# A Mamba-2 and attention trunk on one core: the first group's xs turned by TensorE, and a later place for the second group's turn

## The chip, the cores and the metric

The kernel runs on one NeuronCore of a Trainium2 chip. A core has five engines with a queue each: TensorE (PE in the profile; its weight loads are PEld), VectorE (DVE), ScalarE (ACT), GpSimd (POOL) and SyncE (SP, which only starts DMAs here). Each engine takes its instructions in the order of its queue, and waits for others by semaphores. Matrix products are written to PSUM and must be read from there by DVE or ACT before their buffer is used again. The metric is the device time of one execution in microseconds (us), lower is better; the time of a kernel is the median of its runs.

## The reference

One Mamba-2 layer and one sliding-window attention layer, 256 tokens of width 2048, float32. The change lies in the Mamba-2 layer. Cut to it:

```python
zxbcdt = x @ w_in                      # z, xs, B, C, dt
xbc = silu(conv(xbc) + conv_b)         # 4 taps, for xs, B and C
dt  = softplus(dt_raw + dt_bias)
x_c = xs * dt[..., None]               # tokens x (64 heads x 64), in 8 groups of 8 heads
cb     = einsum("bcqgn,bcsgn->bgcqs", c_c, b_c)
y_diag = einsum("bgcqs,bgrcqs,bcsgrp->bcqgrp", cb, decay_in, x_c)
y = y_diag + y_off + xs * d_skip
y = y * silu(z)
y = y * rsqrt(mean(y * y over the 512 channels of a group) + EPS) * norm_w
h = y @ w_out
x = layernorm(ALPHA * x + h)
```

The sum over `s` (tokens) needs x_c with tokens on the partitions. The projection leaves xs with channels on the partitions, so each group's xs must be turned.

## The kernel before, in words

**Products.** Every weight is split into a high and a low part (`wh` by ACT, L164; `wl` by DVE, L167), x likewise, and a product is three matmuls (L252). Weights come in units of 128 x 2048: SyncE loads two halves into raw buffers `wr`, ACT and DVE split them (`load_unit`, `split_half`), and `next_unit` keeps the loads two units ahead. A raw buffer is free when both splits have read it.

**Groups and blocks.** There are eight groups of ten blocks (`group`, `block`). A block is 48 matmuls into one of four PSUM buffers (`mm`). In group 0 the blocks are z0, z1, z2, b, c, xs0 to xs3, z3; in the others b, c, xs0 to xs3, z0 to z3. So blocks 10, 11 and 12 are bt, ct and xs0 of group 1, and 16 to 19 its z. Each b, c or xs block goes through `conv_silu`: one ACT instruction and three DVE (L492, L494) out of PSUM, a Tanh (L497) and a product (L498). A z block is one ACT (L582) and one DVE (L583) out of PSUM.

**The state-space part of a group.** `cb` makes B times C (L590, L591) and masks it (L592). The decays `e` come from a broadcast load (`load_decay`), from ACT (L549, L557) and a product with cbm on DVE (`by_cb`, L597). `ymm` multiplies e with `xd`, the turned and scaled xs (L631), and DVE takes the result out of PSUM with `el` (L636) and adds the skip (L642). `gate` multiplies by z, squares and sums on GpSimd (L647, L649, L653), and ACT and DVE split y into yH and yL (L661, L662). `norm` sums the squares over the partitions on TensorE (L671); group 0 then takes the root with small DVE instructions (L680 to L687).

**The turn of xs.** `turn_xs` transposes 32 x 32 pieces on DVE, four instructions of 128 x 256 (L604). `carry_xs` moves the pieces to their partitions with 16 ACT copies (L613). `scale_xs` multiplies by dt (L618).

**The output product.** `out_units(g - 1, ...)` runs behind some blocks of group g (`OUT_AT`): for each unit and each half of the tokens 12 matmuls of 512 columns into an `mm` buffer (L323 to L325), which DVE scales by r and adds into `xr` (L332). For group 0 these stand behind blocks 16, 17, 18 and 19.

**The order.** The program is written in blocks. `plan` holds what comes behind a block, `between` what comes behind a block's matmuls but ahead of its evictions; the numbers count blocks from the start (`at(t, fn, ...)`). A scheduler may move instructions within an engine's queue, but those marked `keep_in_program_order` (through `pinned`) keep their order. `visits` names the functions that put other work on TensorE; the block behind one takes its first slice of x from its usual place and not from a copy.

Of the kernel before, what the change touches and what calls it, by code (L numbers as in the profile page):

```python
# [8 lines left out]
F32 = mybir.dt.float32  # L9
# [5 lines left out]
ALU = mybir.AluOpType  # L15
AX = mybir.AxisListType

P = 128
S = 256
# [64 lines left out]
def trunk(ctx: ExitStack, tc: tile.TileContext, A: dict, out: bass.AP, dbg=None):  # L84
    nc = tc.nc
    PSUM = bass.MemoryType.PSUM

    def pool(name, bufs=1, side=None, space=None, stack=ctx):
        kw = {"space": space} if space is not None else {}
        return stack.enter_context(  # L90
            tc.tile_pool(name=name, bufs=bufs, side=side, reuse_waits="tile", **kw)
        )
# [9 lines left out]
    def nm(s):  # L102
        uid[0] += 1
        return f"{s}_{uid[0]}"

    def mm_tile():
        return mm_ps.tile([P, 512], F32, tag="mm", name=nm("mm"), bufs=4)

    def ax_tile():
        return ax_ps.tile([P, 512], F32, tag="ax", name=nm("ax"), bufs=4)  # L110

    cc = cst.tile([P, 1024], F32, tag="cc", name="cc")
    ident = cc[:, 0:128]
# [169 lines left out]
    ap = pool("ap", stack=w_stack)  # L283
# [25 lines left out]
    def pinned(m, pin):  # L309
        if pin:  # L310
            tc.keep_in_program_order(m)
# [86 lines left out]
    dtx = ap.tile([P, 2, NHD], F32, tag="dtx", name="dtx")  # L398
# [163 lines left out]
    gs = [G() for _ in range(NG)]  # L562
# [32 lines left out]
    def by_cb(g, hf):  # L595
        e = es[g, hf]
        nc.vector.tensor_tensor(e[:], e[:], gs[g].cbm[:].unsqueeze(1).to_broadcast([P, 4, 384]), ALU.mult)  # L597

    def turn_xs(g):

        st = gs[g]
        st.zx = ap.tile([P, 4, 8, 32], F32, tag="yz", name=nm("zx"), bufs=1)
        for i in range(4):
            nc.vector.transpose(st.zx[:, i].rearrange("p f b -> p (f b)"), st.xs[i][:])  # L604
        st.xd = ap.tile([P, 2, 4, P], F32, tag="xd", name=nm("xd"), bufs=1)

    def carry_xs(g, js):
# [103 lines left out]
        else:  # L711
            (in_b, in_c)[k](g, ps)

    visits = (turn_dt, cb, ymm, norm)

    def group(g):
        for b in range(10):
# [75 lines left out]
    between = {}  # L793
# [6 lines left out]
    def at(t, fn, *a):  # L800
        plan.setdefault(t, []).append((fn, *a))
# [5 lines left out]
    for g in range(NG):  # L807
        t = 10 * g
        if g == 0:
            at(TD, turn_dt, *dts)  # L810
            at(4, load_decay, 0, 1)
            at(8, load_low, 0)
            pos = dict(cb=CB0, y=13)

            xs_at = 9
            halves = [(5, 6, 7), (7, 8, 9)]
            by = (9, 10)
        elif g == 1:
            at(10, load_decay, 1, 0)
            at(10, load_decay, 1, 1)  # L820
            at(15, load_low, 1)
            pos = dict(cb=6, y=Y_AT, norm=10 + CB_AT)

            halves = [(13, 14, 15), (15, 16, 16)]
            by = (16, 17)
        else:
            at(t - 5, load_decay, g, 0)
            at(t - 5, load_decay, g, 1)
            at(t, load_low, g)
            steps = t - 1  # L830
            pos = dict(cb=CB_AT, y=Y_AT, norm=10 + CB_AT)
        for hf in range(2):
            if g < 2:
                sa, sb, ex = halves[hf]
                if (g, hf) != (1, 0):
                    at(sa, sum_decay, g, hf, 0, 2)
                at(sb, sum_decay, g, hf, 2, 4)
            else:
                at(steps + hf, sum_decay, g, hf)
                ex = steps + 1 + hf  # L840
            at(ex, exp_decay, g, hf)
        if g == 1:
            at(16, norm, 0)
        at(t + pos["cb"], cb, g)
        for hf in range(2):
            at(by[hf] if g < 2 else t + pos["cb"] + hf, by_cb, g, hf)
        if g > 0:
            xs_at = t + 6
        at(xs_at, turn_xs, g)
        if g == 0:  # L850
            at(9, carry_xs, 0, (0,))
            between[10] = [(carry_xs, 0, (1,))]
            between[11] = [(carry_xs, 0, (2, 3)), (scale_xs, 0)]
        else:
            for n, js in enumerate(((0,), (1,), (2, 3)) if g < 2 else ((0, 1), (2, 3))):
                at(xs_at + n, carry_xs, g, js)
            at(xs_at + 2, scale_xs, g)
        at(t + pos["y"], ymm, g)
        if g == 0:
            at(t + pos["y"], sum_decay, 1, 0, 0, 2)  # L860
        for i in range(4):
            at(t + pos["y"], gate, g, i)
        if g > 0:
            at(t + pos["norm"], norm, g)
# [148 lines left out]
    for h in range(2):  # L1013
        ps = mm_tile()
# [449 lines left out]
```

## Time and profile before

| | us |
|---|---|
| median of 3 runs | 986.46 |
| lowest, highest | 985.95, 986.79 |
| profiled execution, its own time | 985.89 |
| its span, first to last instruction | 984.1 |

The granted TensorE clock was 0.999 of full speed. In the profile L12 means line 12 of the kernel. In a timeline a row gives the start from the beginning of the span, the duration, the engine, the line and operation, output<-inputs, shapes, the number of instructions merged, and in brackets the engine's idle time just before and what ended it. Durations of neighbouring instructions overlap; the pace of an engine is the distance between starts. In a row of groups the busy time and the mean in ns of one instruction follow the bar, then the idle time before them. A list of waits has the total, the number and the longest.

### The profile page before, as it was taken

Reading aid. Unit: us, or ns where it says so; the run is one execution under the profiler, and the core shown is the slowest. Engines: PE = TensorE matmul, PEld = TensorE weight load, DVE = VectorE, ACT = ScalarE, POOL = GpSimd, SP = SyncE. Lnnn points to the kernel's source line nnn. Section 1 sums busy time; section 2 is a strip of 40 time slices with the busy share of each in tenths; the row PEclk is TensorE's granted clock in tenths of the full one; section 3 lists DMA queues with packets and bytes.
Section 4 is the critical chain, followed back from the end, with each engine's and each line's share of the span. In section 5 each row is a group of like instructions: output and inputs, shape, how many; then the busy total and the mean of one; then the engine's idle time right before and its main releaser. Section 6 shows DMA issues by size and latency. Waiting matters only on the chain.

```text
span 984.1 us, 18075 instructions
## 1 busy us (share of the span) xinstructions
PE 973.6 (99%) x7004; PEld 883.8 (90%) x7004; DVE 783.3 (80%) x1202; ACT 662.7 (67%) x1236; POOL 103.2 (10%) x137
## 2 busy tenths in 40 slices
PE   9999899999999999999999999999999999999998
PEld 8999889999998999999999999888898978978976
DVE  7888897876878787797788687989867678766786
ACT  7596787667676666657766667467467777764772
POOL 0000403004003000300300300303100000000003
PEclk9999999999999999999999999999999999999999
DMA  9798467566657656656656564648655546464542
GB/s 359 251 292 297 147 230 255 174 208 200 214 172 241 212 190 219 209 169 236 204 175 198 176 216 149 211 166 281 220 163 165 190 157 196 159 208 147 200 143 86
DMA packets 61557, 198.89 MB, mean 202 GB/s; under 512 B 6848, under 2 KB 11360, under 8 KB 61216
## 3 DMA queue, kind: packets, MB, share of 16 engines
q1 hardware_dynamic: 58528, 188.53, 58.0%
q0 software_dynamic: 2336, 8.69, 2.7%
q8 instruction: 55, 0.90, 0.4%
q10 hardware_dynamic: 608, 0.52, 0.2%
q14 instruction: 30, 0.25, 0.1%
HBM read 195.49 MB, written 2.23 MB: 201 GB/s over the span
## 4 chain that ended last, share of the span: by engine, by line
PE 86%; DVE 5%; ACT 4%; DMA 3%; issue 1%; SPq 1%; ACTq 0%; DVEq 0%
PE mm L252 43%; PE mm L984 11%; PE mm L323 9%; PE mm L325 9%; PE mm L324 9%; PE ax L631 2%; DVE wl L167 2%; DMA wr<-in_wa 1%; ACT wh L164 1%; ACT e L549 1%; DMA rb<-rscr 1%; DMA xr<-in_first 1%; ACT xd L613 1%; PE ax L1124 1%; SPq L192 1%
## 5 line engine op out<-in xcount | busy, mean ns | idle before, releaser
L167 DVE TENSOR_TENSOR wl<-wr,wh 128x1024 fp32r<-128x1024 f32 (+2 forms) x338 | 392.8, 1181 | 88.5 <-ACT wh L164 86.6
L164 ACT ACTIVATE wh<-wr 128x1024 fp32r<-128x1024 f32 (+2 forms) x338 | 332.1, 1010 | 92.4 <-PE mm L252 32.7
L252 PE MATMUL mm<-xH,wh 128*128 128x256 f32 x1280 | 355.0, 277 | 0.0
L252 PE MATMUL mm<-xL,wh 128*128 128x256 f32 x1280 | 354.2, 277 | 0.0
L252 PE MATMUL mm<-xH,wl 128*128 128x256 f32 x1280 | 354.0, 277 | 0.0
L252 PEld LDWEIGHTS mm<-xH,wh 128*128 128x128 f32 x1280 | 240.8, 188 | 2.0 <-ACT wh L198 0.3
L252 PEld LDWEIGHTS mm<-xL,wh 128*128 128x128 f32 x1280 | 240.6, 188 | 0.9
L252 PEld LDWEIGHTS mm<-xH,wl 128*128 128x128 f32 x1280 | 240.6, 188 | 0.0
L323 PE MATMUL mm<-wh,yH 128*128 128x512 f32 x256 | 101.3, 396 | 2.4 <-DVE xr L332 2.4
L324 PE MATMUL mm<-wh,yL 128*128 128x512 f32 x256 | 99.8, 390 | 0.0
L325 PE MATMUL mm<-wl,yH 128*128 128x512 f32 x256 | 99.7, 389 | 0.0
L647 POOL TENSOR_TENSOR yz<-yz,z 128x256 f32<-128x256 f32 x32 | 32.7, 1030 | 469.6 <-DVE yz L642 469.6
L494 DVE SCALAR_TENSOR_TENSOR cv<-mm,pc,cv 128x255 f32<-128x255 f32 x144 | 68.4, 476 | 4.5 <-ACT cv L492 3.1
L252 PE MATMUL mm<-x1H,wh 128*128 128x256 f32 x256 | 71.9, 281 | 0.0
L252 PE MATMUL mm<-x1L,wh 128*128 128x256 f32 x256 | 71.1, 278 | 0.0
L252 PE MATMUL mm<-x1H,wl 128*128 128x256 f32 x256 | 71.1, 278 | 0.0
L984 PE MATMUL mm<-wh,x1H 128*128 128x512 f32 x160 | 63.1, 394 | 0.0
L984 PE MATMUL mm<-wl,x1H 128*128 128x512 f32 x160 | 61.8, 389 | 0.0
L984 PE MATMUL mm<-wh,x1L 128*128 128x512 f32 x160 | 60.9, 390 | 0.0
L323 PEld LDWEIGHTS mm<-wh,yH 128*128 128x128 f32 x256 | 48.1, 188 | 13.0 <-DVE xr L332 2.8
L497 ACT ACTIVATE xs<-cv 128x256 f32<-128x256 f32 x32 | 13.3, 415 | 66.8 <-DVE cv L494 66.8
L325 PEld LDWEIGHTS mm<-wl,yH 128*128 128x128 f32 x256 | 48.1, 188 | 10.2
(228 smaller groups left out, 1456.1 us busy)
## 6 DMA issues: line engine op xcount, KB each, us to landing
wr<-in_wa SPq DMA_DIRECT2D x154, 512.0 KB, 5.2
wr<-in_wo SPq DMA_DIRECT2D x64, 512.0 KB, 4.4
wr<-in_wq SPq DMA_DIRECT2D x32, 512.0 KB, 4.5
wr<-in_wg SPq DMA_DIRECT2D x31, 512.0 KB, 5.0
wr<-in_wb SPq DMA_DIRECT2D x16, 512.0 KB, 4.3
wr<-in_wb SPq DMA_DIRECT2D x32, 256.0 KB, 3.8
rb<-rscr SPq DMA_DIRECT2D x11, 512.0 KB, 4.1
wr<-in_wkv SPq DMA_DIRECT2D x8, 512.0 KB, 4.8
```

The lines of the kernel that those rows point to most:

```text
L164: m = nc.scalar.activation(h[:, sl], v, AF.Copy)
L167: m = nc.vector.tensor_tensor(l[:, sl], v, h[:, sl].bitcast(F32), ALU.subtract)
L192: nc.sync.dma_start(raw, A["first"][:, k, :])
L252: m = nc.tensor.matmul(ps, a, b, start=first and i == 0, stop=last and i == 2)
L323: pinned(nc.tensor.matmul(ps, aH[:, k, hs], u.h[:, ks], start=k == 0 and add is None, stop=False), pin)
L324: pinned(nc.tensor.matmul(ps, aL[:, k, hs], u.h[:, ks], start=False, stop=False), pin)
L325: pinned(nc.tensor.matmul(ps, aH[:, k, hs], u.l[:, ks], start=False, stop=k == 3), pin)
L494: nc.vector.scalar_tensor_tensor(a[:, sft:], ps[:, : S - sft], w(3 - sft), a[:, sft:], ALU.mult, ALU.add)
L497: nc.scalar.activation(dst, a[:], AF.Tanh)
L631: nc.tensor.matmul(ps[64 * r : 64 * r + 64, cols], st.xd[:, c, i, 64 * r : 64 * r + 64], e[:, 256:] if c else e[:, :256], start=c == 0, st ...
L647: nc.gpsimd.tensor_tensor(v, v, st.z[i][:], ALU.mult)
L984: m = nc.tensor.matmul(ps[:], (x1H, x1L, x1H)[i][:, kk, hs], (u.h, u.h, u.l)[i][:, ks], start=(kk, i) == (0, 0), stop=ui == 3 and (k, i) = ...
```

## The change

Group 0's `turn_xs`, `carry_xs` and `scale_xs` (behind blocks 9, 10 and 11) go. In their place `turn_first(0)` stands behind the matmuls of block 11: eight 128 x 128 transposes on TensorE into two PSUM buffers, and four DVE instructions that multiply by dt on the way out of PSUM, kept in program order. In group 1 `turn_xs` moves from behind block 16 to between the matmuls and the eviction of block 17, its four transposes kept in program order, and the 16 copies come in two parts behind blocks 17 and 18 in place of three behind 16, 17 and 18. Groups 2 to 7 keep their places. In DVE's built queue group 1's four transposes stand behind the first two L332 and two splits of weights, where before they stood ahead of these L332; the first e product of group 1 stands between the two L332.

```diff
+    def turn_first(g):
+        st = gs[g]
+        st.xd = ap.tile([P, 2, 4, P], F32, tag="xd", name=nm("xd"), bufs=1)
+        for k in range(2):
+            ps = ax_tile()
+            for i in (2 * k, 2 * k + 1):
+                for c in range(2):
+                    o = (i % 2) * S + c * P
+                    nc.tensor.transpose(ps[:, o : o + P], st.xs[i][:, c * P : (c + 1) * P], ident)
+            for i in (2 * k, 2 * k + 1):
+                o = (i % 2) * S
+                hh = g * 8 + 2 * i
+                m = nc.vector.tensor_tensor(
+                    st.xd[:, :, i, :].rearrange("p c (h d) -> p c h d", h=2),
+                    ps[:, o : o + S].rearrange("p (c h d) -> p c h d", c=2, h=2),
+                    dtx[:, :, hh : hh + 2].unsqueeze(3).to_broadcast([P, 2, 2, 64]), ALU.mult,
+                )
+                pinned(m, True)
...
         for i in range(4):
-            nc.vector.transpose(st.zx[:, i].rearrange("p f b -> p (f b)"), st.xs[i][:])
+            m = nc.vector.transpose(st.zx[:, i].rearrange("p f b -> p (f b)"), st.xs[i][:])
+            pinned(m, g == 1)
...
-    visits = (turn_dt, cb, ymm, norm)
+    visits = (turn_dt, cb, turn_first, ymm, norm)
...
-            xs_at = 9
+            between[11] = [(turn_first, 0)]
...
         if g > 0:
             xs_at = t + 6
-        at(xs_at, turn_xs, g)
-        if g == 0:
-            at(9, carry_xs, 0, (0,))
-            between[10] = [(carry_xs, 0, (1,))]
-            between[11] = [(carry_xs, 0, (2, 3)), (scale_xs, 0)]
-        else:
-            for n, js in enumerate(((0,), (1,), (2, 3)) if g < 2 else ((0, 1), (2, 3))):
-                at(xs_at + n, carry_xs, g, js)
+            if g == 1:
+                between[17] = [(turn_xs, 1)]
+            else:
+                at(xs_at, turn_xs, g)
+            for n, js in enumerate(((0, 1), (2, 3))):
+                at(xs_at + n + (g == 1), carry_xs, g, js)
             at(xs_at + 2, scale_xs, g)
```

## The prediction

> **What bounds the kernel now.** I read the busy shares and the chain of waits first, then TensorE's own waits, then the timeline of each engine round them.
>
> ```profile
> PE 973.6 (99%) x7004; PEld 883.8 (90%) x7004; DVE 783.3 (80%) x1202; ACT 662.7 (67%) x1236; POOL 103.2 (10%) x137
> ...
> PE 86%; DVE 5%; ACT 4%; DMA 3%; issue 1%; SPq 1%; ACTq 0%; DVEq 0%
> ```
> TensorE (PE) is the bound. An instruction added to it costs its whole pace, and only its idle time can be won. The list of its waits over the span is short:
>
> ```profile
> PE ax L671 <- POOL sq L653: 2.6, 1, 2.6
> PE mm L323 <- DVE xr L332: 2.4, 1, 2.4
> PE ax L372 <- DVE zero L360: 1.0, 1, 1.0
> ```
> The third is at the start. The other two lie between the first and second group, which is where the change works. TensorE's timeline there (start, duration, line, and the idle time before with its releaser):
>
> ```profile
> 87.20 2.82 PE L631 MATMUL ax<-e,xd 128*64 128x256 f32 x32
> ...
> 106.29 0.28 PE L252 MATMUL mm<-xH,wl 128*128 128x256 f32 x1
> 109.13 0.61 PE L671 MATMUL ax<-cc,sq 128*128 128x1 f32 x4 [2.56 <-POOL sq L653]
> ...
> 115.84 0.35 PE L252 MATMUL mm<-xH,wh 128*128 128x256 f32 x1
> ...
> 121.57 0.39 PE L323 MATMUL mm<-wh,yH 128*128 128x512 f32 x1
> ...
> 124.06 0.39 PE L325 MATMUL mm<-wl,yH 128*128 128x512 f32 x1
> 126.82 0.50 PE L323 MATMUL mm<-wh,yH 128*128 128x512 f32 x1 [2.37 <-DVE xr L332]
> ...
> 129.69 0.28 PE L252 MATMUL mm<-xH,wh 128*128 128x256 f32 x1
> ...
> 146.16 2.82 PE L631 MATMUL ax<-e,xd 128*64 128x256 f32 x32
> ```
> At 87.20 is the ymm of group 0, at 109.13 the norm of group 0, at 115.84 block 17, at 121.57 the second output unit (two halves of 12 matmuls), at 129.69 block 18, at 146.16 the ymm of group 1. The first wait is for GpSimd's sum of squares, the second for a PSUM buffer that L332 must first add into xr.
>
> ```profile
> 98.26 0.73 POOL L647 TENSOR_TENSOR yz<-yz,z 128x256 f32<-128x256 f32 x1 [27.61 <-DVE yz L642]
> ...
> 108.34 0.74 POOL L653 TENSOR_TENSOR sq<-sq,sq 128x256 f32<-128x256 f32 x1
> ```
> GpSimd works from 98.26 to 109.08 and had idled 27.61 us before it: it is late only because VectorE (DVE) reaches the eviction of the ymm (L636) late, at 96.66. DVE's timeline:
>
> ```profile
> 70.13 0.77 DVE L604 STREAM_TRANSPOSE zx<-xs 128x256 f32<-128x256 f32 x2
> ...
> 89.02 0.42 DVE L498 SCALAR_TENSOR_TENSOR ct<-ct,cv 128x256 f32<-128x256 f32 x1 [0.54 <-ACT ct L497]
> ...
> 96.66 0.68 DVE L636 TENSOR_TENSOR yz<-ax,el 128x512 f32<-128x512 f32 x1
> ...
> 114.69 1.00 DVE L494 SCALAR_TENSOR_TENSOR cv<-mm,pc,cv 128x254 f32<-128x254 f32 x2
> ...
> 122.50 0.16 DVE L687 SCALAR_TENSOR_TENSOR r<-r 128x2 f32<-128x2 f32 x1
> 122.58 0.55 DVE L592 TENSOR_TENSOR cbm<-ax,cc 128x384 f32<-128x384 f32 x1
> 123.05 0.43 DVE L604 STREAM_TRANSPOSE zx<-xs 128x256 f32<-128x256 f32 x1
> 123.41 1.72 DVE L597 TENSOR_TENSOR e<-e,cbm 128x1536 f32<-128x1536 f32 x1
> 125.04 1.08 DVE L604 STREAM_TRANSPOSE zx<-xs 128x256 f32<-128x256 f32 x3
> 126.06 1.36 DVE L332 SCALAR_TENSOR_TENSOR xr<-mm,r,xr 128x512 f32<-128x512 f32 x2
> 127.34 2.34 DVE L167 TENSOR_TENSOR wl<-wr,wh 128x1024 fp32r<-128x1024 f32 x2
> ```
> The scale r is ready at 122.66, but one cbm, four transposes and one e product stand ahead of the first L332, which ends near 126.8, when TensorE resumes. Block 17 is released just in time too: the L494 pair that frees its buffer ends at 115.69, and the block starts at 115.84.
>
> **Part 1: eight transposes on TensorE.** They stand behind block 11 (before, TensorE was there at 76). The nearest rows are the eight of L915:
>
> ```profile
> 656.26 1.03 PE L915 MATMUL ax<-cc,xr 128*128 128x128 f32 x8
> 657.05 0.48 PE L323 MATMUL mm<-wh,yH 128*128 128x512 f32 x1
> ```
> Eight with the same shape hold the queue for 0.79 us (656.26 to 657.05): **+0.79**. Their inputs, the xs, are there before the last two L604 read them at 70.13, so TensorE doesn't wait for them. [...] The row shows 1.03 us for eight that overlap, so the pace holds, not the duration.
>
> **Part 2: how much earlier DVE becomes.** Removed from it for group 0 are four transposes and the scaling L618; added are four PSUM evictions of 128x256. Removed from ScalarE (ACT) are 16 copies.
>
> ```profile
> L618 DVE TENSOR_TENSOR xd<-xd,dtx 128x1024 f32<-128x1024 f32 x1 | 1.2, 1226 | 0.6 <-ACT xd L613 0.6
> ...
> L583 DVE SCALAR_TENSOR_TENSOR z<-z,mm 128x256 f32<-128x256 f32 x2 | 0.8, 416 | 0.0
> ```
> ```profile
> 71.51 3.31 ACT L613 COPY xd<-zx 32x256 f32<-32x256 f32 x8
> ...
> 76.88 1.24 ACT L613 COPY xd<-zx 32x256 f32<-32x256 f32 x3
> ...
> 78.73 2.06 ACT L613 COPY xd<-zx 32x256 f32<-32x256 f32 x5
> ```
> ```profile
> core 0: us, PE busy (x) PEld busy (x) DVE busy (x) ACT busy (x) POOL busy (x), PEclk, DMA share, GB/s
> 62.58:89.02 26.44, 26.44 (x240) 25.88 (x241) 23.29 (x34) 23.05 (x44) 0.53 (x1) 1.00 0.84 286
> ```
> Over the stretch that ends with ct's L498 at 89.02, DVE is busy 23.29 us and idle 3.15. Busy work falls by 4 x 0.34 (three L604 and the next instruction start that far apart from 125.04 on) and 1.2, and rises by 4 x 0.4 (L583, the same size out of PSUM): -1.0. Idle time falls because the copies (6.6 us) no longer stand ahead of ACT's splits and conv starts, for which DVE waits; walking both queues in the new order, with starts as far apart as in these rows, I get 2.4 idle (0.9 ahead of the L498 of an xs, 0.4 and 0.1 ahead of a split and an e product, 0.5 each behind the Tanh of bt and ct), so -0.75. DVE leads by **1.75 us** at ct. Its order from there to the norm is unchanged, so GpSimd ends at 109.08 - 1.75 = 107.33. Bounds for the lead: all idle gone, 4.0; below, an eviction can be dearer. L642 shows that:
>
> ```profile
> L642 DVE SCALAR_TENSOR_TENSOR yz<-xs,pc,yz x8: 472/830/2165, 97.6 to 151.9; 128x256 f32<-128x256 f32 x8
> ```
> At its 2.17 the four evictions cost 7.1 more and DVE is 5.3 late. The slow ones run beside GpSimd, which the rows above show idle for 27.61 us until 98.26, so I take 0.4. The evictions wait for TensorE, which is done at 77.1, and DVE comes to them at 81.6: no wait. Queued behind them are the ct convolution and the splits of units 15 and 16. The evictions end near 83.3; the ymm that reads them starts at 88.0. No DMA and no SP or GpSimd instruction changes place; weights load as DVE's L167 frees raw buffers, in this stretch earlier.
>
> **Part 3: the norm wait.** TensorE's last matmul of block 16 starts at 106.29, so it is free at 106.40, now 107.2 with the transposes. The norm waits 0.1 in place of 2.56: **-2.46**. TensorE then leads by 109.13 - 107.33 = 1.8, as DVE does; a bigger TensorE lead would be stopped at block 17 by the L494 pair.
>
> **Part 4: the second output unit.** The four transposes go behind both L332, and the e product stands between these. r is ready at 122.66 - 1.75 = 120.9; cbm takes 0.47 and the first L332 0.75, to 122.05. TensorE asks for the buffer at 122.5 (121.57 - 1.8 and 12 matmuls, 2.73). The wait goes: **-2.37**.
>
> **Part 5: what is late next.** DVE goes on: e product to 123.7, second L332 to 124.4, two splits of block 18's weights to 125.5 and 126.6, four transposes to 128.0, e product to 129.7, a split to 130.8, then z of block 17 (L583) to 131.2. TensorE starts block 18 at 125.2 and needs the first split at 125.4: +0.1. It ends the block at 130.75 and needs the buffer that this z frees: **+0.35**. ACT:
>
> ```profile
> 122.98 2.93 ACT L164 ACTIVATE wh<-wr 128x1024 fp32r<-128x1024 f32 x3
> 126.16 5.39 ACT L613 COPY xd<-zx 32x256 f32<-32x256 f32 x13 [0.25 <-DVE zx L604]
> ```
> It ends these splits at 124.2 and stands until the transposes end, 128.1; behind it wait the z of block 17 (130.1, in time for DVE), an xr scaling, the 16 copies (0.41 each) and block 19's splits, done 133.7 and 134.7. Block 19 starts at 136.6 and waits 0.15 for the L332 behind them. Copies end at 137.9, L618 at 139.1, and the ymm needs it at 142.3, against 146.16: 3.2 us of slack. Together **+0.6**, bounds 0 and 2 (if the copies are handed over as late as ACT's 4 us of idle suggests). From the ymm on TensorE finds everything early, as later groups do.
>
> **Sum:** 0.79 - 2.46 - 2.37 + 0.6 = -3.44. The profiled execution took 985.89 (span 984.1, 1.8 round it), which gives 982.45. That execution lies 0.57 below the median of the runs, 986.46, which gives 983.0.
>
> **Rivals.** *DVE gains no lead.* For: ACT and DVE wait for each other in turn, and idle time may only move. Then the transposes fill part of the norm wait (2.56 to 1.77, net nothing) and only the second wait goes: -2.37 + 0.6, 984.7. [...] *The norm wait doesn't shrink because GpSimd's own chain is the limit*: it is busy for nearly all of its 10.8 us but starts when DVE releases it, so this falls together with the first. *Slower: the evictions are dear.* At L642's median of 0.83 DVE loses its lead; each further us of lateness reaches TensorE at the norm. Break-even is where lateness equals 2.37 - 0.6 = 1.8, an eviction of 0.4 + (1.75 + 1.8)/4 = 1.3 us; at 2.17 the kernel loses 5.3 - 1.8 = 3.5 and takes 990.0. For: source in PSUM, a broadcast factor, strided output. Against: L583 reads PSUM in 0.416, and L618 has the same factor at 1.2 us for four times as much.
>
> **Numbers.** Forecast 0.62 (own range 982.0 to 984.3); no lead, with GpSimd's chain in it, 0.16; dear transposes 0.06; dear evictions 0.16, 0.06 of it within 0.2%. A measurement can tell 0.2%, or 2.0 us, from no change, so faster means under 984.5. Faster: 0.62, 0.05 of the dear transposes and 0.03 of the no-lead case, 0.70; same: the other 0.14 of these two and the 0.06, 0.20; slower: 0.10. The range reaches from 982.0 (both waits gone, no new one: -2.56 - 2.37 + 0.79 on the median, 982.3, and the spread of the runs) past the no-lead case to 985.6.
>
> **What would show it.** TensorE's list of waits: L671 under 0.5, L323 behind L332 gone, a new wait under 0.5 before the output unit after block 18. Eight transposes in 0.8 us, evictions of 0.4. First L647 of GpSimd near 96.5, first L332 near 121.3, ymm of group 1 near 142.3. I am wrong if that ymm starts after 144.5, or if TensorE waits later in group 1 or in group 2 for what ACT does behind its idle time.

## The result, and the profile after

| | us |
|---|---|
| changed kernel, median of 20 runs | 983.22 (981.73 to 985.61) |
| kernel before, median of 20 runs | 986.12 (984.13 to 987.42) |
| ratio, 95% interval | 0.9974 (0.9967 to 0.9981) |
| profiled execution of the changed kernel, its span | 984.83, 982.8 |

The change gains 2.6 us by the ratio and 2.9 by the medians; 983.0 was forecast. The number came out, but not all of its terms did. The profiled execution is one of the longer ones: its span is only 1.3 below that of before. Why that is so is the main thing to learn here.

In the new numbering the eight transposes of `turn_first` are L608, its evictions L612, the 32 x 32 transposes L624 (before, L604), the ACT copies L634 (L613), the scaling L639 (L618), the ymm L652 (L631), its evictions L657 and L663 (L636, L642), GpSimd's steps L668, L670, L674, and the norm L692 (L671). Lines up to L597 are unchanged. The busy shares and the chain of waits of the changed kernel:

```profile
PE 974.9 (99%) x7012; PEld 884.2 (90%) x7012; DVE 781.1 (79%) x1201; ACT 655.6 (67%) x1220; POOL 104.5 (11%) x137
...
PE 82%; DVE 8%; ACT 4%; DMA 3%; issue 2%; POOL 1%; ACTq 0%; SPq 0%; DVEq 0%; POOLq 0%
```

TensorE has eight more instructions, DVE and ACT have less work, and yet DVE's share of the chain rises from 5% to 8%. TensorE's longest waits (total, number, longest):

```profile
PE ax L372 <- DVE zero L360: 1.0, 1, 1.0
PE mm L252 <- DVE xr L332: 0.9, 1, 0.9
PE mm L252 <- DVE wl L167: 0.6, 1, 0.6
PE mm L252 <- ACT wh L198: 0.2, 1, 0.2
PE mm L252 <- DVE cv L494: 0.2, 1, 0.2
```

Both waits that the change works on are gone: the norm's for GpSimd, and the output unit's for L332. The first, third and fourth row lie ahead of 60 us. The other two, for L332 and cv, are in group 2, where the kernel before had none. Counted from start to start these two stops cost 1.67 us, more than the 1.14 of idle time, as the matmuls round a stop are further apart (0.22 us from 192.29 to the next one, where later ones start 0.11 to 0.12 apart). TensorE's timeline of the changed kernel:

```profile
77.01 1.04 PE L608 MATMUL ax<-cc,xs 128*128 128x128 f32 x8
77.80 0.36 PE L252 MATMUL mm<-xH,wh 128*128 128x256 f32 x1
...
120.38 0.39 PE L323 MATMUL mm<-wh,yH 128*128 128x512 f32 x1
...
125.84 0.28 PE L252 MATMUL mm<-xH,wh 128*128 128x256 f32 x1
...
185.65 0.36 PE L252 MATMUL mm<-xH,wh 128*128 128x256 f32 x1 [0.20 <-DVE cv L494]
...
192.29 0.38 PE L252 MATMUL mm<-xH,wh 128*128 128x256 f32 x1 [0.94 <-DVE xr L332]
```

The transposes hold the queue for 0.79 us (77.01 to 77.80). The second output unit runs through from 120.38 to 125.84, 5.46 us, where it took 8.12. Where TensorE stands against before, from the starts of the same work in the two profiles (minus: earlier than before):

| start of | before | after | difference |
|---|---|---|---|
| cb of group 0 (L590) | 59.23 | 60.01 | +0.78 |
| ymm of group 0 | 87.20 | 88.87 | +1.67 |
| norm of group 0 | 109.13 | 108.24 | -0.89 |
| block 18 | 129.69 | 125.84 | -3.85 |
| ymm of group 1 | 146.16 | 143.18 | -2.98 |
| norm of group 1 | 181.71 | 178.73 | -2.98 |
| first output unit of group 2 | 199.17 | 197.86 | -1.31 |

Behind that last row nothing changes any more: 1.3 is the difference of the spans. The first 0.78 is no work of the change, whose first instruction on TensorE starts at 77.01: this execution waited ahead of 60 us where that of before did not. The transposes add the next 0.79. TensorE wins 2.56 us at the norm and 2.96 from there to block 18, and gives back 0.87 before the ymm of group 1 and 1.67 in group 2. DVE of the changed kernel in the stretch that matters:

```profile
82.73 1.41 DVE L612 TENSOR_TENSOR xd<-ax,dtx 128x256 f32<-128x256 f32 x4
...
95.77 0.68 DVE L657 TENSOR_TENSOR yz<-ax,el 128x512 f32<-128x512 f32 x1
...
121.41 0.55 DVE L592 TENSOR_TENSOR cbm<-ax,cc 128x384 f32<-128x384 f32 x1
121.88 0.74 DVE L332 SCALAR_TENSOR_TENSOR xr<-mm,r,xr 128x512 f32<-128x512 f32 x1
...
127.13 1.42 DVE L624 STREAM_TRANSPOSE zx<-xs 128x256 f32<-128x256 f32 x4
...
134.38 2.36 DVE L167 TENSOR_TENSOR wl<-wr,wh 128x1024 fp32r<-128x1024 f32 x2 [0.93 <-ACT wh L164]
...
138.67 1.23 DVE L639 TENSOR_TENSOR xd<-xd,dtx 128x1024 f32<-128x1024 f32 x1 [1.26 <-ACT xd L634]
...
149.74 1.28 DVE L657 TENSOR_TENSOR yz<-ax,el 128x512 f32<-128x512 f32 x2
...
191.49 0.75 DVE L332 SCALAR_TENSOR_TENSOR xr<-mm,r,xr 128x512 f32<-128x512 f32 x1 [0.52 <-ACT r L713]
```

The last two rows in the kernel before:

```profile
149.07 1.28 DVE L636 TENSOR_TENSOR yz<-ax,el 128x512 f32<-128x512 f32 x2
...
190.82 0.75 DVE L332 SCALAR_TENSOR_TENSOR xr<-mm,r,xr 128x512 f32<-128x512 f32 x1 [0.52 <-ACT r L692]
```

And ACT, behind three splits of weights:

```profile
121.81 2.94 ACT L164 ACTIVATE wh<-wr 128x1024 fp32r<-128x1024 f32 x3
128.58 1.65 ACT L634 COPY xd<-zx 32x256 f32<-32x256 f32 x4 [3.84 <-DVE zx L624]
...
135.32 3.31 ACT L634 COPY xd<-zx 32x256 f32<-32x256 f32 x8
```

ACT stands 3.84 us for the late transposes, so DVE later stands 0.93 us for ACT's split and 1.26 for its copies. DVE, 1.17 us ahead of before at cbm (121.41 against 122.58), is 0.67 behind before at the eviction of the ymm of group 1 (149.74 against 149.07): 1.84 us lost. It is still 0.67 behind at the L332 of group 2 for which TensorE then waits until 192.29.

### The profile page after: what moved, and what is told of

Read it like the earlier page. It is cut to its first block, busy times and chain, and to the rows that moved or that the text cites. A ratio compares the mean times of both kernels' runs of the same rounds, so it can differ in the third digit from the quotient of the medians.

```text
span 982.8 us, 18081 instructions
## 1 busy us (share of the span) xinstructions
PE 974.9 (99%) x7012; PEld 884.2 (90%) x7012; DVE 781.1 (79%) x1201; ACT 655.6 (67%) x1220; POOL 104.5 (11%) x137
## 4 chain that ended last, share of the span: by engine, by line
PE 82%; DVE 8%; ACT 4%; DMA 3%; issue 2%; POOL 1%; ACTq 0%; SPq 0%; DVEq 0%; POOLq 0%
PE mm L252 41%; PE mm L1003 11%; PE mm L323 8%; PE mm L324 8%; PE mm L325 8%; DVE wl L167 3%; PE ax L652 2%; ACT wh L164 1%; DMA wr<-in_wa 1%; DVE cv L494 1%; DMA xr<-in_first 1%; DMA rb<-rscr 1%; ACT e L549 1%; PE ax L1143 1%; ACT xd L634 1%
## 5 line engine op out<-in xcount | busy, mean ns | idle before, releaser
L167 DVE TENSOR_TENSOR wl<-wr,wh 128x1024 fp32r<-128x1024 f32 (+2 forms) x338 | 392.7, 1180 | 88.2 <-ACT wh L164 85.8
L323 PE MATMUL mm<-wh,yH 128*128 128x512 f32 x256 | 101.3, 396 | 0.1
L668 POOL TENSOR_TENSOR yz<-yz,z 128x256 f32<-128x256 f32 x32 | 32.7, 1030 | 465.3 <-DVE yz L663 465.3
L497 ACT ACTIVATE xs<-cv 128x256 f32<-128x256 f32 x32 | 13.3, 416 | 68.9 <-DVE cv L494 68.9
L323 PEld LDWEIGHTS mm<-wh,yH 128*128 128x128 f32 x256 | 48.1, 188 | 10.6 <-DVE z L583 1.1
```

The source lines that it names most:

```text
L167: m = nc.vector.tensor_tensor(l[:, sl], v, h[:, sl].bitcast(F32), ALU.subtract)
L323: pinned(nc.tensor.matmul(ps, aH[:, k, hs], u.h[:, ks], start=k == 0 and add is None, stop=False), pin)
L497: nc.scalar.activation(dst, a[:], AF.Tanh)
L668: nc.gpsimd.tensor_tensor(v, v, st.z[i][:], ALU.mult)
```

## The experiments

Two theories of the waits in group 2 were set against each other. *A*: they are the price of the second group's late turn, which lengthens the chain of work that DVE and ACT hand to each other. *B*: they come from a late start of this one execution. Beside that, single terms were doubled, and the cost of an idle TensorE was looked at. Every kernel ran in five rounds beside the kernel before:

| kernel | median us (runs) | ratio to before, 95% | span of its profile |
|---|---|---|---|
| e1, first part alone | 982.62 (12) | 0.9970 (0.9958 to 0.9982) | 984.1 |
| e2, second part alone | 985.45 (11) | 0.9989 (0.9981 to 0.9998) | 984.5 |
| e3, both groups on TensorE | 982.48 (5) | 0.9966 (0.9953 to 0.9979) | 980.3 |
| e4, evictions twice | 983.94 (12) | 0.9978 (0.9965 to 0.9990) | 982.5 |
| e5, transposes twice | 983.53 (10) | 0.9977 (0.9968 to 0.9987) | 981.3 |
| e6, turn ahead of the splits | 981.60 (6) | 0.9958 (0.9944 to 0.9972) | 979.4 |
| e7, e1 with its wait filled | 983.73 (12) | 0.9978 (0.9968 to 0.9987) | 981.7 |
| e8, all groups on TensorE | 987.84 (12) | 1.0021 (1.0010 to 1.0032) | 985.5 |
| changed kernel again | 983.20 (12) | 0.9969 (0.9956 to 0.9981) | 982.9 |
| e6 again | 982.23 (6) | 0.9954 (0.9938 to 0.9969) | 980.7 |
| e1 again | 984.14 (12) | 0.9972 (0.9961 to 0.9983) | 981.0 |
| kernel before again | 985.63 (12) | 0.9992 (0.9980 to 1.0004) | 983.3 |

The spans of single profiles don't stand in the order of the medians. Executions of one kernel differ in when DVE and ACT reach group 0 (called the phase below); the last four runs are there to separate this from the program's order.

**e1, the first part alone.** Group 1's turn and copies as before:

```diff
-            if g == 1:
-                between[17] = [(turn_xs, 1)]
-            else:
-                at(xs_at, turn_xs, g)
+            at(xs_at, turn_xs, g)
```

> Only the first group's turn is changed; the second group's stays where it was before. Both theories: the norm wait (2.56 us before) falls under 0.5, eight transposes take 0.79 on TensorE, the wait of the output matmuls L323 for L332 stays at 2 to 2.6 because VectorE and TensorE lead by about the same 1.8. Chain theory (between the groups VectorE and ScalarE hand work to each other without waiting for TensorE, and their place in time caps TensorE's gain in group 2): VectorE still leads by 1.5 or more in group 2, no new wait there, 1.7 us faster than before, 984.4. Theory of adding terms: 0.79 - 2.46 = -1.7, the same. It tells whether the first part is worth its forecast alone.

Both theories gave it a gain of 1.7, and it gained about 3 by the ratio: its median is that of the whole change, within what can be told. The table of distances below says why. The norm wait is gone; in this execution the wait for L332 is still there. Its timeline of TensorE, and its windows (stretch, length, busy us and instructions of PE, PEld, DVE, ACT, POOL, then granted clock, DMA share, GB/s):

```profile
125.24 0.50 PE L323 MATMUL mm<-wh,yH 128*128 128x512 f32 x1 [2.36 <-DVE xr L332]
...
127.03 0.63 PE L323 MATMUL mm<-wh,yH 128*128 128x512 f32 x1
127.46 0.63 PE L324 MATMUL mm<-wh,yL 128*128 128x512 f32 x1
```
```profile
124.00:126.00 2.00, 0.76 (x3) 0.67 (x4) 2.00 (x5) 1.72 (x5) 0.00 (x0) 1.00 0.30 123
126.00:128.00 2.00, 2.00 (x7) 1.52 (x6) 2.00 (x2) 1.94 (x6) 0.00 (x0) 0.59 0.13 12
128.00:130.00 2.00, 2.00 (x8) 1.62 (x7) 2.00 (x3) 1.93 (x6) 0.00 (x0) 0.55 0.87 260
130.00:132.00 2.00, 2.00 (x20) 2.00 (x19) 1.56 (x3) 2.00 (x3) 0.00 (x0) 1.00 0.74 258
```

Behind the wait the matmuls start 0.43 us apart in place of 0.23, at half the granted clock. From 0.59 and 0.55 in two slices of 2 us follow 1.6 + 1.8 = 3.4 us at half clock, behind a wait of 2.36 us.

**e2, the second part alone.** Without `turn_first`; group 0 is turned by DVE and ACT as before.

```diff
-            between[11] = [(turn_first, 0)]
+            xs_at = 9
...
-    visits = (turn_dt, cb, turn_first, ymm, norm)
+    visits = (turn_dt, cb, ymm, norm)
```

> Only the second group's turn is moved; the first group's stays on VectorE and ScalarE. Adding terms: the norm wait stays at 2.5, the wait for L332 (2.37) goes, 0.6 comes back, so 1.8 us faster than before, 984.4. Chain theory: ScalarE stands idle for about 4 us until the late transposes, VectorE reaches group 2 about 2.4 us later than before, and the slack there is about 2.0 (in the changed kernel VectorE was 0.67 late and TensorE kept 1.31 of its lead), so TensorE waits in group 2 for L332 or L494 until nothing is left: 986.1 to 986.7, no gain.

It gains about 1 us by the ratio (0.2 to 1.9), between the 1.8 of one theory and the nothing of the other. The wait for L332 is gone and the norm waits 2.25. The windows of its profile show half clock behind that, 6.83 us of it, so its span says little:

```profile
105.46:108.87 3.41, 1.44 (x13) 1.24 (x11) 3.38 (x7) 2.00 (x3) 3.40 (x5) 1.00 0.54 154
108.87:112.29 3.42, 3.15 (x10) 2.79 (x11) 3.17 (x5) 1.33 (x3) 0.22 (x1) 0.50 0.47 137
112.29:115.70 3.41, 3.41 (x9) 2.64 (x8) 1.44 (x3) 3.41 (x8) 0.57 (x1) 0.50 0.74 252
```

**e3, both groups on TensorE.** Group 1 is turned like group 0, behind block 17's matmuls; its copies and its scaling go (not shown).

```diff
-                between[17] = [(turn_xs, 1)]
+                between[17] = [(turn_first, 1)]
```

> The second group's xs too are turned by TensorE (eight transposes behind block 17's matmuls, four evictions), without the 16 copies, the four VectorE transposes and the scaling of group 1. Chain theory: ScalarE's idle time before the copies (3.84 in the changed kernel) and VectorE's 1.26 before the scaling go, TensorE waits in group 2 for neither L332 nor L494; TensorE pays another 0.79; in all 0.79 x 2 - 2.46 - 2.37 + 0.2 = -3.05 or a little more, 982.4 to 983.1. Adding terms: the changed kernel's -3.44 with 0.79 more and 0.6 less, -3.25, but then the changed kernel itself should have no wait in group 2 when it starts on time.

TensorE pays another 0.79 and has no wait behind the first microseconds. With five runs the median can't be told from that of the change.

**e4, the evictions twice.** Each L612 is issued twice.

```diff
+                for _ in range(2):
                     m = nc.vector.tensor_tensor(
```

> The changed kernel with each of the four evictions done twice: 1.4 us more on VectorE before ct. Chain theory: the norm wait comes back at about 1.2 to 1.4, block 17 and all of group 1 shift with it, VectorE is 1.4 later in group 2 too, so 1.2 to 1.6 slower than the changed kernel, 984.6. Rival (VectorE has slack there, since it idles 20% of the time): no change, 983.2.

The norm wait that was expected from four more evictions did not come, and no other wait up to 140 us: of their 4 x 0.33 us only 0.38 reach cbm (the table below), the rest falls into DVE's idle time, which shrinks by 0.88 from the phase to cbm. But DVE's queue was built in another order here, with the evictions between steps of the ct convolution, so more than the evictions differs. The median is 0.7 dearer, which the intervals don't separate. At an eviction of 0.83 the prediction has DVE lose its lead; twice 0.41 leaves it 1.9 of 2.3 us at cbm. So that rival would have needed a higher price than the break-even given for it, which is likely but not shown.

**e5, the transposes twice.** Each transpose is issued twice.

```diff
+                    for _ in range(2):
                         nc.tensor.transpose(ps[:, o : o + P], st.xs[i][:, c * P : (c + 1) * P], ident)
```

> Each of the first group's eight transposes is issued twice, into the same place: 0.79 us more on TensorE behind block 11. Adding terms: 0.79 slower than the changed kernel, 984.0. Chain theory: the 0.79 replaces waiting later on (at the norm, at block 18, in group 2), so that group 2's waits are 0.79 shorter and the end does not move: 983.2, within 0.3.

Sixteen hold the queue for 1.66 us, about twice the 0.79. The profiled execution nevertheless spans 1.5 us less than that of the changed kernel, as DVE reached group 0 earlier in it; its wait in group 2 is 0.4. The median, 983.53, lies between the two forecasts and decides nothing.

**e6, the second group's turn ahead of the splits.** The four transposes stand directly behind the two L332, and the two splits of block 18's weights behind them (the call goes to the top of `block`, ahead of `next_unit`).

```diff
+        if (g, b) == (1, 7):
+            turn_xs(1)
         u = next_unit()
...
-                between[17] = [(turn_xs, 1)]
```

> The changed kernel with the second group's four transposes directly behind the two L332, ahead of the two splits of block 18's weights. Chain theory: ScalarE's idle time before its copies falls from 3.8 to about 1.5, VectorE's 1.26 before the scaling goes, block 18 waits 1.3 longer for its low weights, and group 2's waits (1.7 in the changed kernel's profile) shrink by about as much: 982.6 to 983.4. Adding terms: block 18's longer wait is paid in full, 984.5.

It is the fastest of all, and the interval of its ratio lies below that of e2, e8 and 1, and overlaps that of the change only in part.

**The changed kernel, e6, e1 and the kernel before, again**, on one chip.

> The changed kernel once more, unaltered, for a second profile. Phase theory: what TensorE waits for in group 2 is set by the landing of a DMA near 57 us, ahead of ScalarE's L164. If the first L332 starts before 120.5 (VectorE's L167 near 59), the waits of group 2 are shorter than the 1.67 us of the first profile, by what VectorE is earlier (0.0 to 0.5 left when it is 1.5 us earlier), and the time is 981.7 to 983. If it starts after 121.5, they are 1.3 to 1.8 and the time 984 to 985.5. Chain theory without phase (the waits are in the program's order alone): 1.3 to 1.8 of waits in group 2 whenever L332 starts. Median 983.2.

> The kernel with the second group's turn ahead of block 18's splits, unaltered, on one chip with the changed kernel. If the order of the turn is what it gains: 1.0 to 1.8 us below the changed kernel run beside it (median 981.4 to 982.2), and no wait of TensorE over 0.4 us behind 120 us also when the first L332 starts after 121. If the 981.6 of its first runs was a chip or a phase: the same median as the changed kernel within 0.5, and waits in group 2 of 1 us or more where L332 is late.

> The first group's turn on TensorE alone, unaltered, for a second profile. Clock theory: in an execution whose mean clock is 0.999 or more the wait for L332 is below 2.3 us, as VectorE is earlier there, and no slice is below full clock; such executions take 981 to 983.4 and the others 985.4 to 986.6. Rival: the wait is 2.3 to 2.5 in all of them and the half clock comes by chance. Median 982 to 984.

> The kernel before, unaltered, for a second profile. Clock theory: two of three executions have a mean clock of 0.998 or less; if the profiled one does, its trace shows a stretch of about 3.4 us at half clock behind one of the two waits of over 2 us, and no other stretch below full clock between 60 and 980 us. If it does not, both waits are there at full clock as in the first profile. Rival: the lower clock lies elsewhere and has nothing to do with the two waits. Median 986.1.

The changed kernel's profile came out like the first one: L332 at 121.83, a wait of 0.9 in group 2, 984.93 us; the norm waits 0.28. An early execution of it was not caught. e6 gained 0.97 on it, just short of the 1.0 expected, and with six runs this isn't clear of the spread; over both of its batches it has 981.85 (12 runs) against 983.22 (32 runs of the changed kernel). It has a wait of 0.53 us, above the 0.4 expected, as block 18's splits now stand behind the turn. e1's wait for L332 was 0.72 this time, with no slice below full clock, as the clock theory says. But three of its runs at a mean clock of 0.999 took 984.5 to 985.0, above the range given, so the clock is not all that spreads them. The kernel before had both waits, 1.98 and 2.5, at full clock.

Three rows answer A against B: DVE's cbm of group 1 (L592), ACT's third Tanh for xs in group 2 (L497), and TensorE's first output unit of group 2 (L323). From the timelines of the kernel before (its cbm starts at 122.58), of the changed kernel, of e5 and of e6 again:

```profile
191.99 0.42 ACT L497 ACTIVATE xs<-cv 128x256 f32<-128x256 f32 x1 [0.26 <-DVE cv L494]
...
199.17 0.39 PE L323 MATMUL mm<-wh,yH 128*128 128x512 f32 x1
```
```profile
121.41 0.55 DVE L592 TENSOR_TENSOR cbm<-ax,cc 128x384 f32<-128x384 f32 x1
...
192.66 0.42 ACT L497 ACTIVATE xs<-cv 128x256 f32<-128x256 f32 x1 [0.26 <-DVE cv L494]
...
197.86 0.39 PE L323 MATMUL mm<-wh,yH 128*128 128x512 f32 x1
```
```profile
119.37 0.55 DVE L592 TENSOR_TENSOR cbm<-ax,cc 128x384 f32<-128x384 f32 x1
...
190.62 0.42 ACT L497 ACTIVATE xs<-cv 128x256 f32<-128x256 f32 x1 [0.26 <-DVE cv L494]
...
195.82 0.39 PE L323 MATMUL mm<-wh,yH 128*128 128x512 f32 x1
```
```profile
120.16 0.55 DVE L592 TENSOR_TENSOR cbm<-ax,cc 128x384 f32<-128x384 f32 x1
...
190.22 0.42 ACT L497 ACTIVATE xs<-cv 128x256 f32<-128x256 f32 x1 [0.25 <-DVE cv L494]
...
195.54 0.39 PE L323 MATMUL mm<-wh,yH 128*128 128x512 f32 x1
```

From cbm to the Tanh the changed kernel takes 71.25 us, and its near twin e5, where DVE is 2.04 us earlier, takes 71.25 as well. The same distances for the profiles, with DVE's phase (the start of the last L167 pair near 60 us) ahead of them:

| profile | phase | phase to cbm | cbm to Tanh | Tanh to output unit |
|---|---|---|---|---|
| before, before again | 60.31, 59.56 | 62.27, 62.28 | 69.41, 69.41 | 7.18, 7.16 |
| e2 | 60.32 | 62.28 | 71.25 | 5.46 |
| e1, e1 again | 61.04, 59.43 | 59.96, 59.76 | 70.65, 69.40 | 7.52, 7.18 |
| e7 (e1 with its wait filled, below) | 60.21 | 60.00 | 69.44 | 7.14 |
| after, after again | 61.42, 61.40 | 59.99, 59.96 | 71.25, 71.25 | 5.20, 5.20 |
| e4, e5 | 60.45, 58.88 | 60.34, 60.49 | 71.25, 71.25 | 5.20, 5.20 |
| e6, e6 again | 58.81, 60.20 | 59.75, 59.96 | 70.10, 70.06 | 5.83, 5.32 |
| e3 | 59.22 | 59.78 | 68.86 | 7.52 |

The first part makes DVE 2.3 us earlier at cbm in every phase (62.28 to 60.00 or less; 1.8 to 1.9 in e4 and e5, which add to it). The second part costs the chain of DVE and ACT 1.84 us (69.41 to 71.25), with the first part or without it. (e1's 70.65 is the execution with half clock; e1 again and e7, with the same order at full clock, have 69.40 and 69.44.) And where the last column has 5.20, TensorE starts at a fixed distance behind the Tanh: there this chain sets the time, not TensorE's own work. The kernel before had 7.18 - 5.20 = 1.98 us of slack. So TensorE can gain up to there 1.98 plus what the chain gains, and no more. For the profile after: the chain's -2.28 and +1.84, and a phase 1.11 later, are +0.67 together, and 1.98 - 0.67 = 1.31 is the gain. For e5: the Tanh is 1.37 earlier than in before, and TensorE's gain there is 3.35 (199.17 to 195.82), again 1.98 more. Order (A) and phase (B) both count, and add up.

The three distances of a row add up to TensorE's place behind the phase: 138.86 and 138.85 for before, 136.44 and 136.41 for after, 136.34 for e1 again, 136.58 for e7, 136.16 for e3, 135.68 and 135.34 for e6. So, with the phase taken out, the change gains 2.4 us, e1 again 2.5, e7 2.3, e3 2.7 and e6 3.2 to 3.5. This is why e1 does as well as the whole change: its TensorE resumes when DVE comes to L332, so it gains what DVE gains and not the 1.7 of its own terms, and its wait follows the phase (2.36 us at 61.04, 0.72 at 59.43). The second part then spends 1.84 of the 1.98 us that it frees. By that it should be worth 0.14 alone too, while e2 gained 0.2 to 1.9 by its ratio; where the rest comes from stays open (e2's one profile, with its half clock, has 138.99).

**e7, e1 with its wait filled.** Ten matmuls whose result nobody reads stand in the second output unit where TensorE waits for L332.

```diff
+                    if (g, nb, h) == (0, 1, 1):
+                        ps = ax_tile()
+                        for _ in range(10):
+                            pinned(nc.tensor.matmul(ps[:], gs[g].y[0][:, 0, :P], u.h[:, :512], start=True, stop=True), True)
```

> The first part alone (as e1_first_only), and ten matmuls of 512 columns, whose result nothing reads, in TensorE's queue where it waited 2.4 us for L332. They keep TensorE busy, and cost 2.27 us, no more than the wait. Clock theory (in some executions the idle 2.4 us bring half clock for 3.4 us after it, as in the profiles of e1_first_only and e2_second_only): no execution at a mean clock of 0.998 or less (4 of 12 in e1_first_only, at 985.5 to 986.6), all within 981 to 983.7, median 982.3. Rival (the slow executions of e1_first_only come from the start of the program or from DMA): a third of the executions stay at 985.5 or more.

3.4 us at half clock cost a mean over 984 us some 1.7 / 984, which brings it to 0.998. None of e7's 12 runs had a mean clock that low, against 4 of 12 in e1 and 20 of 28 of the kernel before beside e1. But the filler takes 2.55 us always, and the wait can be as short as 0.72: the median is 983.73 where 982.3 was expected, and the kernel is no better for it.

**e8, all groups on TensorE.**

```diff
-            if g == 1:
-                between[17] = [(turn_xs, 1)]
-            else:
-                at(xs_at, turn_xs, g)
...
+            between[17 if g == 1 else t + 7] = [(turn_first, g)]
```

> All eight groups turned by TensorE: 56 more transposes than in the changed kernel, without the 112 copies, 28 VectorE transposes and seven scalings. The later groups show no wait of TensorE in the profile, so what VectorE and ScalarE save is not on the path: against e3_both_te (982.5) six more groups at 0.79, 4.7 slower, 987.2. Rival (less work on VectorE and ScalarE lets TensorE's small stalls shrink): 984 to 986.

Slower than before: in groups 2 to 7 there is no wait to be won, and the eight transposes of each group hold TensorE for 0.79. Against e3 six groups cost 5.4 us by the medians, 0.9 each, where 0.79 each was expected.

## Why the prediction was right

*The bound* was read rightly for the kernel before. In the changed kernel it holds only up to the cap above: e5 adds 0.87 us to TensorE, and its output unit of group 2 still starts 5.20 behind the Tanh.

*Part 1*, +0.79 for the transposes: measured 0.79. The pace held, not the full duration (272 ns for one of them, or 2.2 us for eight), and L608 waited for nothing.

*Part 2*, DVE's lead: 1.75 forecast. Corrected for the 1.11 of phase it was 2.00 at ct (88.13 against 89.02), from 1.20 less busy and 0.80 less idle time where 1.0 and 0.75 were forecast. It was still 2.00 at the eviction of the ymm (95.77 against 96.66), and 2.28 at cbm. The evictions took 0.41 each where 0.4 was forecast, but start 0.33 apart, and so cost less than four times 0.4. GpSimd's first L668 came at 97.32; less the 1.11 that is 96.2, forecast near 96.5.

*Part 3*, the norm wait, -2.46: measured -2.56 (+1.67 to -0.89). *Part 4*, the second output unit, -2.37: it became 2.66 shorter (8.12 to 5.46), since the first matmuls behind a wait are further apart too (0.33 us to the second in place of 0.23). L332 came at 121.88, 120.77 less the 1.11; forecast near 121.3.

*Part 5* is the term that was mis-sized. It has the right mechanism: ACT idles for the late transposes, the output unit behind block 18 waits for z, block 19 a little. To the ymm of group 1 it gave 0.6, and 0.87 came: by the starts on TensorE 0.19 in block 18, 0.34 at the output unit and 0.35 at block 19, where 0.1, 0.35 and 0.15 were forecast. Its last sentence, "From the ymm on TensorE finds everything early, as later groups do", failed: another 1.67 came in group 2. I had put the question to the ymm, which has slack, and not to the chain of DVE and ACT behind it. The turn makes this 1.84 us longer, where it has 1.98 us of slack less TensorE's own gain. A wait "in group 2 for what ACT does behind its idle time" was named as what would make the forecast wrong, and in the profiled executions it is there.

*The number* held partly by luck, since two misses cancel. The profiled execution gains 1.3 of the 3.44 forecast; in the phase of the profile of before the cap leaves 1.98 + 2.28 - 1.84 = 2.4. Against that, the kernel before pays in most of its runs for a clock that drops, which the sum didn't contain: beside e1 its runs with a mean clock of 0.998 or less have a median of 986.43, the others 985.56. Of the 20 runs of the changed kernel one had such a clock. How much of the 2.6 to 2.9 measured is the clock's is an argument from these medians, not a separate measurement.

*The rivals.* No lead (2.00 came) and dear evictions (0.41) are refuted by the rows above; so GpSimd's chain as the limit falls too. No run shows the dear transposes, to which the numbers give 0.06: one lasts 272 ns in L915 of the kernel before and in L608 alike, but eight held the queue for 0.79 us both times, and sixteen for 1.66 in e5.

*What the second part is worth.* Over all runs the change has 983.22 (32 runs) and the first part alone 983.41 (24): no difference that can be told. On top of the first it makes the chain of DVE and ACT the bound. e6 keeps more of it: there the transposes start 3.45 us behind cbm in place of 5.72, and the chain is 0.67 longer than before in place of 1.84. e6 beats the kernel before clearly; over the changed kernel it leads by 1.4 over all runs and by 0.97 on one chip, with ratios whose intervals still overlap.

## What to carry to other kernels

Before an instruction is moved behind others on a helper engine, follow the chain of engines that hand work to each other up to every place where the bounding engine meets it, the next group included, and hold the delay against the slack there: what is won beyond that slack comes back as a wait. Where executions of one kernel differ by as much as a change is worth, compare the distance between two instructions of one chain, not absolute times; here it was the same to 0.05 us wherever nothing else held the chain up. A wait of over 2 us on TensorE can cost more than its length: with those of e1 (2.36 us) and e2 (2.25 us) came 3.4 and 6.8 us at half clock. It need not, as none came with the wait of 2.56 us in the kernel before (next section).

## What the runs showed of the hardware

Half clock came with waits of 2.36 us (e1) and 2.25 us (e2), but not with those of 2.56 and 2.37 us in the first profile of before, nor 1.98 and 2.5 in its second. So the length alone doesn't decide; what does was not shown. In e1 the granted clock is 0.50 for 3.42 us, and that starts 1.1 us after its wait has ended at 125.24. In e2 it is 0.50 for 6.83 us (the rows stand above), and that starts 0.27 us before its wait ends at 109.14. In the first profile of before it is full for 976.21 us on end, which hold both waits. The wait of e1 with the stretch behind it, and the two waits of the second profile of before:

```profile
122.96:126.37 3.41, 1.13 (x5) 0.95 (x6) 3.41 (x7) 3.11 (x7) 0.00 (x0) 1.00 0.46 174
126.37:129.79 3.42, 3.42 (x10) 2.65 (x9) 3.42 (x4) 3.33 (x9) 0.00 (x0) 0.50 0.51 143
```
```profile
105.00:110.00 5.00, 3.02 (x23) 2.73 (x22) 4.96 (x8) 1.71 (x2) 3.33 (x5) 1.00 0.55 157
110.00:115.00 5.00, 5.00 (x23) 3.97 (x22) 2.73 (x5) 4.80 (x9) 0.57 (x1) 1.00 0.69 213
...
120.00:125.00 5.00, 3.54 (x20) 2.71 (x18) 4.72 (x16) 5.00 (x6) 0.55 (x1) 1.00 0.81 292
125.00:130.00 5.00, 3.93 (x22) 3.43 (x23) 5.00 (x7) 4.62 (x13) 0.00 (x0) 1.00 0.25 70
```

Why half clock lasted twice as long in e2 as in e1 is not shown either.

DVE's phase near 60 us lay between 58.81 and 61.42 over these profiles, a spread as large as the change's gain. Shortly before, ACT stands for two loads, the broadcast for the decays and one of raw weights; in the timelines of the changed kernel and of e6:

```profile
51.11 1.20 ACT L549 ACTIVATE e<-rb,rtk 128x256 f32<-128x256 f32 x3 [5.01 <-DMA rb<-rscr]
...
59.69 1.06 ACT L164 ACTIVATE wh<-wr 128x1024 fp32r<-128x1024 f32 x1 [1.27 <-DMA wr<-in_wa]
```
```profile
49.02 1.20 ACT L549 ACTIVATE e<-rb,rtk 128x256 f32<-128x256 f32 x3 [3.32 <-DMA rb<-rscr]
...
56.82 1.06 ACT L164 ACTIVATE wh<-wr 128x1024 fp32r<-128x1024 f32 x1 [0.49 <-DMA wr<-in_wa]
```

The same ACT work starts 2.09 us apart behind the first load and 2.87 behind the second. What makes these transfers land at different times stays open.
